# Seven output products of a conv-and-MLP block: 512 + 256 columns into one bank each, gate and residual in one VectorE step

## The chip, the cores and the metric

One Trainium2 core of one chip runs the whole block: batch 1, 256 tokens, model width 2048, all in float32. The metric is the device time of one execution in microseconds, as the median of several runs. Beside it a profiled execution of the same program is given; its span is counted from the first to the last instruction of the program.

## The reference

With depth 1 only the convolution mixer runs; the two attention mixers of the file are never called. Cut to what is computed:

```python
cond = silu(c)
sh1, sc1, g1, sh2, sc2, g2 = split(cond @ mod_w + mod_b, 6)
h = rms_norm(x, norm1_g) * (1 + sc1) + sh1
u = h @ conv_w_in + conv_b_in            # 2048 -> 4096
a, gt = split(u, 2);  u = a * sigmoid(gt)
u = causal depthwise convolution of 31 taps (u) + conv_dw_b
u = silu(layer_norm(u) * conv_ln_g + conv_ln_b)
y = u @ conv_w_out + conv_b_out          # 2048 -> 2048
x = x + (1 + g1) * y
h = rms_norm(x, norm2_g) * (1 + sc2) + sh2
x = x + (1 + g2) * (square(relu(h @ mlp_w1)) @ mlp_w2)
```

The change concerns the two lines with `conv_w_out` and `(1 + g1)`.

## The kernel before, in words

**Layout.** Activations are held transposed: 16 tiles of 128 channels by 256 tokens, two tiles to a "pair" (`k2`, eight pairs). A float32 operand is split into a rounded high part and the remainder, low part, both in the format `fp32r`. `hl[k2]` holds for each of its two tiles 512 columns: 256 of the high part, then 256 of the low part. A weight tile of 1 MB is split the same way into two halves, `hi` on ScalarE (L236) and `lo` on VectorE or GpSimd (L240). A product is then high·high + high·low + low·high.

**Jobs.** The block is a list of jobs: 16 `in` jobs (projection into the convolution), eight `out` jobs (the projection of the changed lines), then the MLP. Each `out` job makes two tiles of 128 output channels (`c` = 0, 1). The first, `out` 0, goes through the pairs in the outer loop (`mm_pair`, L283 to L286), so that it can start as soon as the first pair of the layer-normed activation exists, and it writes an `mm` tile of PSUM. The other seven take the function `mm` with `merged` true (L264 to L266): per tile and 128 input channels three products of 256 columns each, all added up in the same 256 columns. Both tiles of such a job share one `acc` tile of PSUM, a bank of 512 columns; there are two `acc` banks, so that one job can be read out while the next is computed. The `in` jobs and the first two `up` jobs use `mm` without `merged` (L268, L269): one product of 512 columns and one of 256 that is added to the second half, which leaves two halves to be added at the end.

**Evacuation of an `out` job (L1405 to L1416).** ScalarE applies gate and bias in place in PSUM, one instruction a tile (L1415: `acc` times the column `mcol(G1, k)` plus `gb`, where `gb` is the gate times `conv_b_out`). VectorE adds the 128x512 residual pair (L1416: `xp` = `acc` + `xp`). The residual `x` is loaded again for this (2 MB, key `("x", 0)`) when the memory of the convolution is free. Then ScalarE squares it (L1418), scales it into `a` (L1427), and `split_act` (L251 on ScalarE, L254 on VectorE) makes `xa[i]`, the operand of the first `up` jobs.

**What makes the operand.** In the stretch just before, ScalarE and VectorE turn the convolution's result into `hl`, pair by pair: VectorE L1386 multiplies by the inverse deviation, ScalarE L1390 applies the SiLU twice (one per tile), then the high part is copied (L251 on ScalarE, or L253 on VectorE for pairs 1 and 5) and VectorE makes the low part (L254).

**What sets the order.** Each engine works through its own list of instructions in order. The lists are written by a scheduler at build time, from its own estimate of times and from priorities: what is under `urgent()` goes ahead of what isn't, and `issue_after` names single instructions that must come first. So a change of the source can move instructions that it doesn't touch. Into the gaps of VectorE the scheduler puts the row sums of the SH2 modulation (L665, two per weight tile, against a copy of `cond` in PSUM) and the `lo` splits of the last `out` and the first `up` weights; GpSimd makes the `lo` parts of `out` 1 to 5.

**Loads.** All weight tiles go through SP's queue in one fixed order and land in seven `raw` buffers; a buffer is free again when its tile is split or summed.

Of the kernel before, what the change touches and what calls it, by code (L numbers as in the profile page):

```python
# [11 lines left out]
AF = mybir.ActivationFunctionType  # L12
ALU = mybir.AluOpType
# [3 lines left out]
T = 256  # L17
# [70 lines left out]
def conv_block(ctx: ExitStack, tc: tile.TileContext, x, vec, dwq, c_row, mod_r, mod_t, mod_c, w_first, w_in, w_out, w1, w2, out):  # L88
# [63 lines left out]
    def urgent():  # L152
        return tc.high_priority(offset=URGENT)
# [102 lines left out]
    def mm(p, c, key, acts_of, ks=range(KT), merged=False):  # L256
        halves = parts[key]
        for k in ks:
            hi, lo = halves[k // HALF]
            m = acts_of[k // 2][:, k % 2, :]  # L260
            if merged:
                out_p, begin, end = p[:, c, 0:T], k == 0, k == KT - 1
                w = hi[:, k % HALF, :]
                nc.tensor.matmul(out_p, w, m[:, 0:T], start=begin, stop=False)  # L264
                nc.tensor.matmul(out_p, w, m[:, T : 2 * T], start=False, stop=False)  # L265
                state["mm_end"] = nc.tensor.matmul(out_p, lo[:, k % HALF, :], m[:, 0:T], start=False, stop=end)  # L266
                continue
            nc.tensor.matmul(p[:, c, :], hi[:, k % HALF, :], m, start=(k == 0), stop=(k == KT - 1))  # L268
            state["mm_end"] = nc.tensor.matmul(  # L269
                p[:, c, T : 2 * T], lo[:, k % HALF, :], m[:, 0:T], start=False, stop=(k == KT - 1),  # L270
                skip_group_check=True,
            )
# [25 lines left out]
    def mm_tokens(sums, job, acts_of, last):  # L298
        steps = [(k, r) for k in range(HALF) for r in sums]
        if last:  # L300
            steps = [(k, r) for r in sums for k in range(HALF)]
        for k, (t, cs, p) in steps:
            hi, lo = [w[:, 4 * (k % 2) : 4 * (k % 2) + 4, :].rearrange("p k n -> p (k n)")[:, cs]
                      for w in parts[job + (k // 4,)][k // 2 % 2]]
            at = HALF * (job[2] % 2) + k
            m = acts_of[at // 2][:, at % 2, :]
            shared = job[0] == "down" and job[1] in EIGHT
            begin, end = at == 0 or shared and job[2] == 1 and t == 1 and at == HALF, at == KT - 1
            p_hi, p_lo = [m[:, n : n + P] for n in (t * P, T + t * P)]
            nc.tensor.matmul(p, p_hi, hi, start=begin, stop=False, skip_group_check=shared)  # L310
            nc.tensor.matmul(p, p_hi, lo, start=False, stop=False, skip_group_check=shared)  # L311
            nc.tensor.matmul(p, p_lo, hi, start=False, stop=end, skip_group_check=shared)  # L312

    def run_tasks():
        state["job"] += 1
        with tc.issue_after(state["w_lo"]), tc.issue_after(state["w_hi"]):
            for task in tasks.pop(state["job"], []):
                task()
# [371 lines left out]
    def mcol(which, k):  # L690
        return modc[:, which * KT + k : which * KT + k + 1]
# [21 lines left out]
    def ps_two():  # L713
        return ps.tile([P, 2, T], F32, name="acc", bufs=2)
# [90 lines left out]
    def splits(job):  # L805
        if job[0] == "eight":
            with urgent():
                split_eight(*job[1:])
            return
        if job[0] == "seven":  # L810
            with urgent():
                split_seven(*job[1:])
            return
        for c in range(2):
            if job + (c,) in parts_early:
                continue
            on_pool = job[0] == "in" or job in POOLED
            with urgent(), behind(c):
                split_w(job + (c,), nc.gpsimd if on_pool else nc.vector)
            if c == 0:  # L820
                state["next_hi"] = state["w_hi"]
                if job[0] in ("up", "down"):
                    with urgent():
                        run_tasks()

    def evac(p, cs=slice(0, 2), out=None):
        t1 = two()[:, cs, :]
# [347 lines left out]
    for n, job in enumerate(jobs):  # L1175
# [49 lines left out]
                    top_up()  # L1225
            continue
        if kind == "out" and i > 0:
            p = ps_two()
        elif not by_tokens(job):
            p = ps.tile([P, 2, 2 * T], F32, name="mm", bufs=2)  # L1230
        if by_tokens(job) and (i % 2 == 0 or kind == "down" and job[1] in EIGHT and i < 4):
# [2 lines left out]
        if job == ("up", 0, 0):  # L1234
            mm(p, 0, job + (0,), xa, range(SIDE))
            for at in range(2 * UNSCALED):
                shift_row(at, shown.pop(("up", 0, at // 2, at % 2)))
            fold_shift()
            mm(p, 0, job + (0,), xa, range(SIDE, KT))
            mm(p, 1, job + (1,), xa)  # L1240
        elif job == ("out", 0):
            for k2 in range(HALF):
                with tc.issue_after(state["row_end"].ins) if k2 == 1 else ExitStack():
                    mm_pair(p, job, k2)
                if k2 == 0:
                    with tc.issue_after(state["mm_end"].ins):
                        mod_chunk(*last_row[0][1:], last_row[1])
        elif job in K_OUTER:
            for k2 in range(HALF):
                for c in range(2):  # L1250
                    mm(p, c, job + (c,), xa if plain else hl, range(2 * k2, 2 * k2 + 2))
        elif kind == "in":
            rows = [key for key in after[job] if key[0] != "col"] if i < KT - 1 else []
            for c in range(2) if i < KT - 1 else (1, 0):
                for ks in (range(HALF), range(HALF, KT)):
                    with tc.issue_after(state.pop("rows_end")) if "rows_end" in state else ExitStack():
                        mm(p, c, job + (c,), hl, ks, i == KT - 1)
            if not CONV_AT.get(n):
                with tc.issue_after(state["mm_end"].ins):
                    mods(rows)  # L1260
                state["rows_end"] = state["row_end"].ins
        elif by_tokens(job):
            mm_tokens(sums[kind, i // 2], job, u2 if kind == "down" else hl, n == len(jobs) - 1)
        else:
            for c in range(2):
                mm(p, c, job + (c,), hl, merged=kind == "out")
        with tc.issue_after(state["mm_end"].ins) if kind == "in" else ExitStack():
            mod_finish()
        if n == KT - 3:
# [136 lines left out]
        if kind == "out":  # L1406
            if i == 0:
                xs = take(("x", 0))
            t2 = p[:, :, 0:T]
            xp = pair_of(xs, i)  # L1410
            with urgent():
                for c in range(2):
                    k = 2 * i + c
                    with tc.issue_after(state["next_hi"]) if i == HALF - 2 else ExitStack():
                        nc.scalar.activation(t2[:, c, :], t2[:, c, :], AF.Identity, scale=mcol(G1, k), bias=gb[:, k : k + 1])  # L1415
                nc.vector.tensor_tensor(xp, t2, xp, op=ALU.add)  # L1416
            ss = two()
            nc.scalar.activation(ss, xp, AF.Square)  # L1418
            if i == 0:
# [162 lines left out]
```

## Time and profile before

| | |
|---|---|
| runs | 1067.75 us median of 3 (1067.61 to 1067.9) |
| profiled execution | span 1065.8 us, 15587 instructions |
| median less span | 1.95 us, around the program's first and last instruction |
| HBM | 313.71 MB read, 17.83 MB written |
| `out` jobs 1 to 7 on TensorE | from 297.9 us; the three lines start 224 times each, the first at 297.8, the last at 380.5 us |
| end of the stage before (SiLU, L1390) | 14 instructions from 286.5 to 296.4 us |

The columns of the views are these. In the timeline: start and duration in us, engine, line, operation, tile written and tiles read, shape, count, and in brackets the idle time of the engine before it with what ended it. In the table by stretch: for each engine busy time and number of instructions, then the granted TensorE clock (1.00 is full), the share of time in which the DMA engines were busy, and GB/s. Durations of successive instructions overlap a little, on TensorE a great deal: what an instruction costs there is the distance between two starts. The names in the profile are those of the first tile in a buffer: a second use of the buffer of `x` is `x` too, and `u` stands for the operand of the MLP.

### The profile page before, as it was taken

Reading aid. Unit: us, or ns where it says so; the run is one execution under the profiler, and the core shown is the slowest. Engines: PE = TensorE matmul, PEld = TensorE weight load, DVE = VectorE, ACT = ScalarE, POOL = GpSimd, SP = SyncE. Lnnn points to the kernel's source line nnn. Section 1 sums busy time; section 2 is a strip of 40 time slices with the busy share of each in tenths; the row PEclk is TensorE's granted clock in tenths of the full one; section 3 lists DMA queues with packets and bytes.
Section 4 is the critical chain, followed back from the end, with each engine's and each line's share of the span. In section 5 each row is a group of like instructions: output and inputs, shape, how many; then the busy total and the mean of one; then the engine's idle time right before and its main releaser. Section 6 shows DMA issues by size and latency. Waiting matters only on the chain.

```text
span 1065.8 us, 15587 instructions
## 1 busy us (share of the span) xinstructions
PE 1048.6 (98%) x5844; PEld 867.4 (81%) x5844; DVE 911.9 (86%) x1176; ACT 609.0 (57%) x841; POOL 220.2 (21%) x153
## 2 busy tenths in 40 slices
PE   6999999999999999999999999999999999999998
PEld 3888886678699998888888888888888888888886
DVE  5767789998766889878879899899999899899896
ACT  4111298866775587444546575745566744657751
POOL 0000078989689262000000000000000000000001
PEclk8999999999999999999999999999999999999999
DMA  9999997997999977999994998693989795899753
GB/s 383 420 420 421 415 419 310 359 397 261 382 401 404 405 247 285 324 334 313 324 359 178 340 269 284 238 382 109 383 241 308 252 331 183 289 304 341 203 146 60
DMA packets 154334, 331.01 MB, mean 311 GB/s; under 512 B 88465, under 2 KB 114321, under 8 KB 119313
## 3 DMA queue, kind: packets, MB, share of 16 engines
q1 hardware_dynamic: 153248, 328.30, 84.8%
q0 software_dynamic: 864, 1.57, 1.1%
q8 instruction: 46, 0.75, 0.3%
q14 instruction: 30, 0.25, 0.1%
q10 hardware_dynamic: 146, 0.13, 0.0%
HBM read 313.71 MB, written 17.83 MB: 311 GB/s over the span
## 4 chain that ended last, share of the span: by engine, by line
PE 83%; DMA 10%; DVE 5%; ACT 1%; issue 1%; SPq 0%; DVEq 0%; ACTq 0%
PE mm L312 12%; PE mm L310 12%; PE mm L311 12%; DMA raw<-mod_c 9%; PE mm L268 6%; PE mm L269 3%; PE acc L265 3%; PE acc L264 3%; PE acc L266 3%; PE mm L1090 2%; PE row L576 2%; PE acc L485 2%; PE acc L486 2%; PE acc L484 1%; DVE raw L669 1%; DVE lo L240 1%
## 5 line engine op out<-in xcount | busy, mean ns | idle before, releaser
L236 ACT ACTIVATE hi<-raw 128x1024 fp32r<-128x1024 f32 x374 | 384.8, 1055 | 258.2 <-PE mm L312 127.6
L240 DVE TENSOR_TENSOR lo<-raw,hi 128x1024 fp32r<-128x1024 f32 x313 | 371.7, 1219 | 52.6 <-ACT hi L236 51.4
L240 POOL TENSOR_TENSOR lo<-raw,hi 128x1024 fp32r<-128x1024 f32 x61 | 153.6, 2549 | 31.1 <-ACT hi L236 31.1
L669 DVE SCALAR_TENSOR_TENSOR raw<-raw,cond 128x2048 f32<-128x2048 f32 x50 | 117.7, 2356 | 27.0 <-DMA raw<-mod_c 26.9
L460 POOL DMA_DIRECT2D out<-two x6 | 5.4, 902 | 641.6 <-DVE two L458 632.3
L311 PE MATMUL mm<-lo,u 128*128 128x512 f32 x320 | 124.5, 389 | 0.0
L312 PE MATMUL mm<-hi,u 128*128 128x512 f32 x320 | 124.0, 389 | 0.0
L310 PE MATMUL mm<-hi,u 128*128 128x512 f32 x320 | 123.8, 389 | 0.0
L312 PE MATMUL mm<-hi,hl 128*128 128x512 f32 x288 | 112.1, 389 | 0.0
L311 PE MATMUL mm<-lo,hl 128*128 128x512 f32 x288 | 112.0, 389 | 0.0
L310 PE MATMUL mm<-hi,hl 128*128 128x512 f32 x288 | 112.0, 389 | 0.0
L969 DVE SCALAR_TENSOR_TENSOR acc<-u,v,acc 128x256 f32<-128x256 f32 x230 | 91.5, 482 | 0.0
L268 PE MATMUL mm<-hl,hi 128*128 128x512 f32 x224 | 80.0, 401 | 0.0
L311 PEld LDWEIGHTS mm<-lo,u 128*128 128x128 f32 x320 | 60.1, 188 | 12.6
L312 PEld LDWEIGHTS mm<-hi,u 128*128 128x128 f32 x320 | 60.1, 188 | 12.5
L310 PEld LDWEIGHTS mm<-hi,u 128*128 128x128 f32 x320 | 60.1, 188 | 12.4
L873 PE MATMUL mm<-two,first 128*128 128x256 f32 x240 | 57.0, 392 | 8.5 <-ACT two L931 8.5
L264 PE MATMUL acc<-hl,hi 128*128 128x256 f32 x224 | 63.4, 283 | 0.0
L265 PE MATMUL acc<-hl,hi 128*128 128x256 f32 x224 | 63.4, 283 | 0.0
L266 PE MATMUL acc<-hl,lo 128*128 128x256 f32 x224 | 63.4, 283 | 0.0
L312 PEld LDWEIGHTS mm<-hi,hl 128*128 128x128 f32 x288 | 54.1, 188 | 11.3
L311 PEld LDWEIGHTS mm<-lo,hl 128*128 128x128 f32 x288 | 54.1, 188 | 11.2
(381 smaller groups left out, 2059.2 us busy)
## 6 DMA issues: line engine op xcount, KB each, us to landing
raw<-w SPq DMA_DIRECT2D x128, 1024.0 KB, 7.3
raw<-mod_c SPq DMA_DIRECT2D x64, 1024.0 KB, 9.7
raw<-mod_r SPq DMA_DIRECT2D x28, 1024.0 KB, 8.8
raw<-w_in SPq DMA_DIRECT2D x16, 1024.0 KB, 10.5
raw<-w_out SPq DMA_DIRECT2D x16, 1024.0 KB, 8.0
first<-w_first SPq DMA_DIRECT2D x15, 1024.0 KB, 19.8
u<-kept SPq DMA_DIRECT2D x24, 512.0 KB, 7.6
flat<-two SPq DMA_DIRECT2D x30, 256.0 KB, 6.9
```

The lines of the kernel that those rows point to most:

```text
L236: state["w_hi"] = nc.scalar.activation(hi, w[:, ks, :], AF.Copy).ins
L240: end = by.tensor_tensor(lo, w[:, ks, :], hi.bitcast(F32), op=ALU.subtract)
L264: nc.tensor.matmul(out_p, w, m[:, 0:T], start=begin, stop=False)
L265: nc.tensor.matmul(out_p, w, m[:, T : 2 * T], start=False, stop=False)
L266: state["mm_end"] = nc.tensor.matmul(out_p, lo[:, k % HALF, :], m[:, 0:T], start=False, stop=end)
L268: nc.tensor.matmul(p[:, c, :], hi[:, k % HALF, :], m, start=(k == 0), stop=(k == KT - 1))
L310: nc.tensor.matmul(p, p_hi, hi, start=begin, stop=False, skip_group_check=shared)
L311: nc.tensor.matmul(p, p_hi, lo, start=False, stop=False, skip_group_check=shared)
L312: nc.tensor.matmul(p, p_lo, hi, start=False, stop=end, skip_group_check=shared)
L669: end = nc.vector.scalar_tensor_tensor(w, w, 1.0, cb, op0=ALU.mult, op1=ALU.mult, accum_out=acc)
L873: step = nc.tensor.matmul(held[n][:, c, :], w[:, 2 * n + c, :], h, start=k == 0 and c == 0, stop=k == KT - 1, skip_group_check=True)
L969: end = nc.vector.scalar_tensor_tensor(out, s, w, acc, op0=ALU.mult, op1=ALU.add)
```

## The change

The seven jobs `out` 1 to 7 no longer use the merged form. Each tile gets an `acc` bank of its own (so a job takes both banks), filled by one product of 512 columns and one of 256. VectorE then reads both halves: two instructions a tile, four a job, each of 128x256, that multiply a half with the gate column as scalar and add it to the residual. The bias part of the sum goes into the residual ahead of time: ScalarE adds `gb` to the fourteen tiles of `x` that belong to these jobs, in fourteen instructions of 128x256 written at `out` 0 to `out` 6, outside `urgent()`. `out` 0 keeps its evacuation. The name `next_hi`, with which the evacuation of `out` 6 was held back, goes away.

```diff
-            if c == 0:
-                state["next_hi"] = state["w_hi"]
-                if job[0] in ("up", "down"):
-                    with urgent():
-                        run_tasks()
+            if c == 0 and job[0] in ("up", "down"):
+                with urgent():
+                    run_tasks()
...
         if kind == "out" and i > 0:
-            p = ps_two()
+            p = [ps_two().rearrange("p a t -> p (a t)")[:, None, :] for _ in range(2)]
...
+        elif kind == "out":
+            for c in range(2):
+                mm(p[c], 0, job + (c,), hl)
         else:
             for c in range(2):
-                mm(p, c, job + (c,), hl, merged=kind == "out")
+                mm(p, c, job + (c,), hl)
...
-            t2 = p[:, :, 0:T]
             xp = pair_of(xs, i)
+            for c in range(2) if i + 1 < HALF else ():
+                k = 2 * i + 2 + c
+                x_next = pair_of(xs, i + 1)[:, c, :]
+                nc.scalar.activation(x_next, x_next, AF.Identity, bias=gb[:, k : k + 1])
             with urgent():
-                for c in range(2):
-                    k = 2 * i + c
-                    with tc.issue_after(state["next_hi"]) if i == HALF - 2 else ExitStack():
-                        nc.scalar.activation(t2[:, c, :], t2[:, c, :], AF.Identity, scale=mcol(G1, k), bias=gb[:, k : k + 1])
-                nc.vector.tensor_tensor(xp, t2, xp, op=ALU.add)
+                if i == 0:
+                    t2 = p[:, :, 0:T]
+                    for c in range(2):
+                        nc.scalar.activation(t2[:, c, :], t2[:, c, :], AF.Identity, scale=mcol(G1, c), bias=gb[:, c : c + 1])
+                    nc.vector.tensor_tensor(xp, t2, xp, op=ALU.add)
+                for c in range(2) if i else ():
+                    for a in range(2):
+                        nc.vector.scalar_tensor_tensor(
+                            xp[:, c, :], p[c][:, 0, T * a : T * a + T], mcol(G1, 2 * i + c), xp[:, c, :],
+                            op0=ALU.mult, op1=ALU.add,
+                        )
```

In the lists of the engines this moves instructions at two places that matter here. In the rows, a number behind a name tells one tile from another, `x1` is the residual that was loaded again, `hl_2621`, `hl_2630`, `hl_2648` are the activation's pairs 3, 4 and 6, `acc_2625` is the SiLU of pair 4, and xN is a count.

ScalarE, where the activation's pairs are made, before:

```order
L1390 ACTIVATE acc_2616<-two_2615,v_72 128x256 x2
L251 ACTIVATE hl_2621<-acc_2616 128x2x256
L1390 ACTIVATE acc_2625<-two_2624,v_72 128x256 x2
L251 ACTIVATE hl_2630<-acc_2625 128x2x256
L1390 ACTIVATE acc_2634<-two_2633,v_72 128x256 x2
L1390 ACTIVATE acc_2643<-two_2642,v_72 128x256 x2
L251 ACTIVATE hl_2648<-acc_2643 128x2x256
```

ScalarE, the same place in the change (L1391 is the SiLU now, L1414 the new bias step):

```order
L1391 ACTIVATE acc_2616<-two_2615,v_72 128x256 x2
L251 ACTIVATE hl_2621<-acc_2616 128x2x256
L1391 ACTIVATE acc_2625<-two_2624,v_72 128x256
L1414 ACTIVATE x1_2504<-x1_2504,gb_2501 128x256 x4
L1391 ACTIVATE acc_2625<-two_2624,v_72 128x256
L1414 ACTIVATE x1_2504<-x1_2504,gb_2501 128x256 x10
L251 ACTIVATE hl_2630<-acc_2625 128x2x256
L1391 ACTIVATE acc_2634<-two_2633,v_72 128x256 x2
L1391 ACTIVATE acc_2643<-two_2642,v_72 128x256 x2
L251 ACTIVATE hl_2648<-acc_2643 128x2x256
```

All fourteen bias steps stand in one place, ahead of the high part of pair 4 and of all that is made after it.

VectorE, around the evacuation of the fifth merged job (`out` 5), before; the three sums of the SH2 modulation around it are two rows each:

```order
L665 SCALAR_TENSOR_TENSOR raw_3226,modc_116<-raw_3226,mm_2942 128x1024
L665 SCALAR_TENSOR_TENSOR raw_3226,rest2_2502<-raw_3226,mm_2944 128x1024
L1416 TENSOR_TENSOR x1_2504<-acc_3392,x1_2504 128x512
L665 SCALAR_TENSOR_TENSOR raw_3230,modc_116<-raw_3230,mm_2942 128x1024
L665 SCALAR_TENSOR_TENSOR raw_3230,rest2_2502<-raw_3230,mm_2944 128x1024
L254 TENSOR_TENSOR u2_3499<-two_3496,u2_3499 128x2x256
L665 SCALAR_TENSOR_TENSOR raw_3240,modc_116<-raw_3240,mm_2942 128x1024
L665 SCALAR_TENSOR_TENSOR raw_3240,rest2_2502<-raw_3240,mm_2944 128x1024
```

VectorE, the same sums in the change, with the evacuation of the second tile of `out` 5 (`acc_3283`) among them:

```order
L665 SCALAR_TENSOR_TENSOR raw_3144,modc_116<-raw_3144,mm_2916 128x1024
L665 SCALAR_TENSOR_TENSOR raw_3144,rest2_2502<-raw_3144,mm_2918 128x1024
L665 SCALAR_TENSOR_TENSOR raw_3148,modc_116<-raw_3148,mm_2916 128x1024
L665 SCALAR_TENSOR_TENSOR raw_3148,rest2_2502<-raw_3148,mm_2918 128x1024
L1423 SCALAR_TENSOR_TENSOR x1_2504<-acc_3283,modc_116,x1_2504 128x256
L665 SCALAR_TENSOR_TENSOR raw_3158,modc_116<-raw_3158,mm_2916 128x1024
L665 SCALAR_TENSOR_TENSOR raw_3158,rest2_2502<-raw_3158,mm_2918 128x1024
L1423 SCALAR_TENSOR_TENSOR x1_2504<-acc_3283,modc_116,x1_2504 128x256
```

The two halves of one bank are now taken with two sums between them, and two whole sums stand ahead of the first.

## The prediction

> **What bounds the kernel now.** I read the page first, then the table by stretch, then the chain of waits and the timelines around the `out` jobs.
>
> ```profile
> PE 1048.6 (98%) x5844; PEld 867.4 (81%) x5844; DVE 911.9 (86%) x1176; ACT 609.0 (57%) x841; POOL 220.2 (21%) x153
> PE 83%; DMA 10%; DVE 5%; ACT 1%; issue 1%; SPq 0%; DVEq 0%; ACTq 0%
> ```
>
> TensorE is busy 98% of the span and carries 83% of the chain that ends last. The table by stretch says whether that holds where the change works and behind it (columns: stretch, length, then PE, PEld, DVE, ACT, POOL busy, clock, DMA share, GB/s):
>
> ```profile
> 305.00:316.00 11.00, 11.00 (x94) 11.00 (x94) 6.58 (x18) 10.21 (x15) 11.00 (x5) 1.00 0.96 386
> 328.00:340.00 12.00, 12.00 (x103) 12.00 (x102) 7.78 (x12) 7.22 (x12) 12.00 (x8) 1.00 1.00 406
> 352.00:364.00 12.00, 12.00 (x103) 12.00 (x102) 11.41 (x17) 7.55 (x11) 1.49 (x2) 1.00 1.02 421
> 364.00:376.00 12.00, 12.00 (x103) 12.00 (x102) 8.57 (x9) 6.36 (x11) 2.64 (x2) 1.00 0.82 311
> 400.00:1060.00 660.00, 659.83 (x2919) 545.25 (x2918) 590.18 (x605) 379.39 (x440) 12.66 (x9) 1.00 0.82 273
> ```
>
> In the `out` jobs TensorE never idles, and from 400 to 1060 us it idles 0.17 us. So a microsecond that TensorE gains or loses at the `out` jobs reaches the end whole: no later wait gives it back. VectorE is nearly full in one stretch (11.41 of 12).
>
> Just ahead of this, where the activation's pairs are made, the chain leaves TensorE. Its rows (start, length, what) and the start of pair 4 on TensorE:
>
> ```profile
> 291.42 0.47 ACT acc L1390
> 291.91 0.58 ACT acc L1390
> 292.51 0.60 ACT hl L251
> ...
> 294.21 0.70 DVE hl L253
> 294.95 0.39 PE mm L285
> ```
> ```profile
> 293.21 0.34 PE L285 MATMUL mm<-hl,hi 128*128 128x256 f32 x1
> ```
>
> ScalarE finishes the high part of pair 4 at 292.51 + 0.60 = 293.11, and TensorE starts pair 4 at 293.21. There is no slack there: ScalarE sets TensorE's pace, and pair 5 waits again, until 294.95.
>
> **The change, part by part.**
>
> *1. The products.* Six steps of the unmerged form in an `in` job and later in an `up` job, and one step of the merged form:
>
> ```profile
> 230.05 0.40 PE L268 MATMUL mm<-hl,hi 128*128 128x512 f32 x1
> ...
> 232.17 0.40 PE L268 MATMUL mm<-hl,hi 128*128 128x512 f32 x1
> ```
> ```profile
> 399.85 0.39 PE L268 MATMUL mm<-u,hi 128*128 128x512 f32 x1
> ...
> 401.93 0.39 PE L268 MATMUL mm<-u,hi 128*128 128x512 f32 x1
> ```
> ```profile
> 300.09 0.28 PE L264 MATMUL acc<-hl,hi 128*128 128x256 f32 x1
> ...
> 300.45 0.28 PE L264 MATMUL acc<-hl,hi 128*128 128x256 f32 x1
> ```
>
> Merged, a step costs 0.360 us; unmerged 2.12 / 6 = 0.353 in the `in` job, 2.08 / 6 = 0.347 in the `up` job. The columns streamed are the same 768; only one instruction's fixed part goes. There are 7 jobs x 2 tiles x 16 steps = 224, so the saving is 224 x 0.0067 = **1.5 us**, or 3.0 at the `up` job's pace. I take 1.5: the `in` jobs run with the same operand `hl`. As bounds, a gain of 0 (the new first step of each bank may lag) to 3.0.
> The Trainium skill, "TensorE: Matmul & The Clock Gate", Part 1, gives a back-to-back distance of N / 2.4 GHz plus a fixed 2.5 ns or so; by that, one matmul fewer saves 224 x 2.5 ns = 0.56 us, an estimate from that page. The rows here show more for a 256-column product (0.120 us against that page's 0.109), so the rows stand.
>
> *2. The fourteen bias steps.* They stand in ScalarE's list between the two SiLUs of pair 4 and its high part, and they need the residual and `gb`:
>
> ```profile
> 282.25 0.37 SPq L212 DMA_DIRECT2D x<-x  x1
> ```
> ```profile
> x<-x SPq DMA_DIRECT2D x1, 2048.0 KB, 12.5
> ```
> ```profile
> L1356 DVE TENSOR_TENSOR gb<-modc,v x1: 175/175/175, 278.3 to 278.3; 128x16 f32<-128x16 f32 x1
> ```
> ```profile
> 335.02 1.11 ACT L1415 ACTIVATE acc<-acc,gb,modc 128x256 f32<-128x256 f32 x2 [4.72 <-PE acc L266]
> 336.06 1.05 ACT L236 ACTIVATE hi<-raw 128x1024 fp32r<-128x1024 f32 x1
> ```
> ```profile
> 319.17 0.90 ACT L1427 ACTIVATE two<-x,amp 128x256 f32<-128x256 f32 x2
> ```
>
> `gb` is there at 278.5. The load of `x` is issued at 282.25 and lands 12.5 us later, at 294.75. Nothing ahead of that differs between the two programs' lists, so I keep this time. ScalarE waits in order: at 335.02 it had stood 4.72 us for a product, with weight splits queued behind. So it reaches the first bias step at 291.9 and stands until 294.8, with pair 4's second SiLU, its high part, pairs 5 to 7, the next weights' `hi` parts (for which GpSimd waits) and the copy of `cond` queued behind.
>
> Then the price of the steps. The same shape on the same tile, L1427, takes 0.90 us for two with 0.495 each, so 0.405 from start to start. Four steps end at 294.8 + 1.6 = 296.4, the SiLU takes 0.58, ten more take 4.05: pair 4's high part starts at 301.1 instead of 292.5. **TensorE stands 8.6 us longer.** If a step costs as L1415 does (1.11 for two, 0.56 apart), 14 x 0.155 = 2.2 us more. Below, it is 14 x 0.405 + 0.1 = 5.8, if `x` had landed before 291.9. TensorE has no other work to take meanwhile: its list goes on with pairs 4, 5 and 6, and only then with `out` 1.
>
> *3. The clock after that stand.* The only long idle time of TensorE in this trace, and the stretches behind it:
>
> ```profile
> 19.71 5.71 PE L873 MATMUL mm<-two,first 128*128 128x256 f32 x16 [4.69 <-ACT two L931]
> ```
> ```profile
> 17.00:19.70 2.70, 0.00 (x0) 0.00 (x0) 2.50 (x8) 0.61 (x2) 0.00 (x0) 0.50 1.01 419
> 19.70:23.80 4.10, 4.09 (x10) 3.28 (x11) 4.06 (x5) 0.41 (x1) 0.00 (x0) 0.50 1.01 422
> 23.80:27.00 3.20, 3.20 (x17) 2.81 (x16) 1.35 (x4) 1.02 (x2) 0.00 (x0) 1.00 1.00 417
> ```
>
> After 4.69 us without work the granted clock was 0.50, and it stayed there for 4.1 us of work (10 matmuls in 4.10 us, then 17 in 3.20). An idle time of over 8 us should do the same: half of 4.1 us is lost, 2.05. Of that, the 0.3 us by which pair 5 waited before is covered now: **+1.7 us**. Bounds: 0 to 3.
> The Trainium skill states the rule behind it ("TensorE: Matmul & The Clock Gate", Part 1: after an idle window of about 3.4 us the clock halves, and comes back after about as long of sustained work); this trace agrees with 4.69 us idle and 0.50 granted.
>
> *4. Evacuation.* Out go fourteen L1415 and seven L1416; in come 28 VectorE steps. The nearest row with PSUM in, a scalar column and SBUF in is L1108:
>
> ```profile
> L1108 DVE SCALAR_TENSOR_TENSOR u<-mm,v,two 128x256 f32<-128x256 f32 x12 | 5.7, 481 | 3.3 <-ACT two L1106 3.2
> L1416 DVE TENSOR_TENSOR x<-acc,x 128x512 f32<-128x512 f32 x7 | 4.8, 686 | 6.3 <-ACT acc L1415 6.3
> L665 DVE SCALAR_TENSOR_TENSOR raw<-raw,mm 128x1024 f32<-128x1024 f32 x24 | 28.1, 1211 | 2.5 <-ACT mm L1437 2.5
> ```
>
> 28 x 0.481 - 7 x 0.686 = 8.7 us more on VectorE, which has 0.6 to 4.4 us free in the stretches above. A job now holds both banks, so the next job's first tile can start only when this job's first tile is read out, half a job (16 x 0.353 = 5.7 us) after its end. Mostly that is enough. The place to fear is `out` 5's second tile: ahead of its first half stand two sums of two rows (4 x 1.2), and between its halves another (2 x 1.2). My count, an estimate on the times of the trace before: VectorE reads `out` 5's first tile at 352 to 354 between splits, starts the sums at about 356, and with 4 x 1.15 + 0.4 + 2 x 1.15 + 0.4 = 7.7 us (rows overlap a little) frees the bank at 363.7. The merged products end at 380.8, and a job took 96 x 0.120 = 11.5, so the second tile of `out` 6 began at 380.8 - 1.5 x 11.5 = 363.5, and at the new pace wants its bank some 0.7 sooner. Behind the waiting instruction stand the `lo` splits of `out` 7 and the first `up` job, with the same small reserve at `out` 6's second tile. I take **+0.8 us** for these waits, with 0 (the loads run ahead during the stand, so sums start earlier) and 3 (each of three tiles late by a whole 1.2 us sum) as bounds. ScalarE's 14 x 0.53 us fewer are off the path: they were covered by TensorE's 100%.
>
> *Sum:* -1.5 + 8.6 + 1.7 + 0.8 = +9.6 us. On the profiled span, 1065.8 + 9.6 = 1075.4; 1.95 us lie around the span (1067.75 - 1065.8), so **1077.3 us**, 0.9% slower.
>
> **The rivals.**
> - *ScalarE has room after all: faster.* If TensorE still gets pair 4 by 293.2, only the products count: 1067.75 - 1.5 = 1066.3. It decides at 291.9: `x` would have to land before it, and 5.7 us of reserve would have to lie between ScalarE and pair 4. For it speaks that ScalarE is busy 57% over all; against it the 0.10 us between 293.11 and 293.21, and the 12.5 us of the load. 4%. A half-way house (`x` early and half of the steps covered, +3 - 1.5) ends within 0.2%: 4%.
> - *The stand, but at full clock.* 1077.3 - 1.7 = 1075.6. For: only one such row in the trace. Against: that row, at half the idle time. 18%.
> - *VectorE becomes the bound.* If in every job both late banks cost a sum (14 x 1.2 less the reserve), 5 to 10 us come on top: 1082 to 1087. For: 11.41 of 12 us busy in one stretch and 8.7 us more work. Against: GpSimd's contention-free stretch after 352, and loads that have run ahead. 8%.
> - *Forecast*, the sum as it stands: 66%.
>
> **How the numbers follow.** Lowest: gain 3.0, stand 8.0 (`x` landing 0.6 us sooner), clock 0, waits 0: +5.0, 1072.8. Highest: gain 0, stand 10.8, clock 1.7, waits 2: +14.5, 1082.2. That range holds the forecast, the full-clock rival and a little of the third. A measurement can tell about 0.2% (2.1 us) from no change. Slower by more: 66 + 18 + 8 = 92%; within: 4%; faster: 4%.
>
> **What would show it.** Right: fourteen L1414 in one row of ScalarE with the first waiting about 2.9 us for `x`; an idle time of some 8.5 us on TensorE before pair 4, named after `hl`; a clock below 1.00 in the 4 us after it; `out` steps of 0.353 us; idle times under 1 us on TensorE at the second tiles of `out` 6 and 7. Wrong: TensorE at pair 4 by 294, or `x` landing elsewhere than at 295; or steps of L1423 far from 0.48 us, or idle time of TensorE at every change of bank; or idle time behind 400 us, where I count none.

## The result, and the profile after

| | before | after |
|---|---|---|
| median | 1067.75 us (1067.34 to 1067.9, five runs) | 1077.97 us (1077.44 to 1087.58, five runs) |
| ratio after / before | | 1.0111, 95% interval 1.0094 to 1.0128 |
| span of the profiled execution | 1065.8 us | 1085.8 us |

The changed kernel is 1.1% slower. Its profiled execution happens to be the longest of the five; the spans of the other four are 1075.7 to 1076.2 us. It holds two events, one that comes back in the second profile of this kernel (e0) and one that doesn't, and they must be read apart. The page (busy times, then the shares of the chain that ended last):

```profile
PE 1050.9 (97%) x5620; PEld 858.1 (79%) x5620; DVE 932.4 (86%) x1197; ACT 607.2 (56%) x841; POOL 220.1 (20%) x153
PE 79%; DVE 9%; DMA 9%; ACT 1%; issue 1%; POOL 0%; SPq 0%; DVEq 0%; ACTq 0%
```

TensorE has 224 products fewer and is nevertheless busy 2.3 us longer, and the chain has moved 4 points from TensorE to VectorE. The timelines of ScalarE where the activation's pairs are made, and of TensorE at pair 4 and at `out` 3's first tile, in this execution:

```profile
291.22 0.56 ACT L1391 ACTIVATE acc<-two,v 128x256 f32<-128x256 f32 x1
294.70 1.70 ACT L1414 ACTIVATE x<-x,gb 128x256 f32<-128x256 f32 x4 [2.91 <-DMA x<-x]
296.31 0.55 ACT L1391 ACTIVATE acc<-two,v 128x256 f32<-128x256 f32 x1
296.80 4.08 ACT L1414 ACTIVATE x<-x,gb 128x256 f32<-128x256 f32 x10
```
```profile
301.41 0.58 PE L285 MATMUL mm<-hl,hi 128*128 128x256 f32 x1 [8.14 <-ACT hl L251]
...
340.99 0.76 PE L268 MATMUL acc<-hl,hi 128*128 128x512 f32 x1 [8.72 <-DVE x L1423]
```

The first idle time is the one that was forecast: ScalarE waits 2.91 us for the residual, then makes fourteen bias steps, and TensorE gets pair 4 at 301.41 instead of 293.21. The second, at 340.99, is the extra of this execution. The table by stretch shows what each does to the clock (the number before the DMA share):

```profile
293.00:301.40 8.40, 0.27 (x3) 0.07 (x1) 0.01 (x1) 6.70 (x17) 0.00 (x0) 0.78 1.02 422
301.40:304.50 3.10, 3.09 (x14) 3.09 (x15) 2.40 (x4) 3.00 (x6) 0.00 (x0) 0.51 1.00 418
304.50:308.00 3.50, 3.50 (x29) 3.41 (x28) 0.36 (x1) 3.47 (x6) 1.74 (x1) 1.00 0.82 335
...
332.30:341.00 8.70, 0.01 (x1) 0.04 (x1) 8.70 (x5) 1.00 (x1) 6.61 (x4) 0.67 0.52 217
341.00:345.40 4.40, 4.40 (x14) 3.72 (x15) 4.37 (x9) 1.33 (x3) 0.00 (x0) 0.50 0.30 56
```

After each of the two idle times TensorE works 3.1 to 4.4 us at half clock: 14 matmuls in 3.09 us, then 29 in 3.50. In the stretch 332.30 to 341.00 VectorE is busy for all 8.70 us, with five instructions. What they are stands in the timelines of VectorE and GpSimd of this execution:

```profile
325.85 13.61 DVE L254 TENSOR_TENSOR u<-two,u 128x512 fp32r<-128x512 f32 x1
339.38 0.47 DVE L1423 SCALAR_TENSOR_TENSOR x<-acc,modc,x 128x256 f32<-128x256 f32 x1
```
```profile
325.82 4.79 POOL L240 TENSOR_TENSOR lo<-raw,hi 128x1024 fp32r<-128x1024 f32 x2
330.55 0.76 POOL L1433 TENSOR_TENSOR sqacc<-sqacc,two 128x256 f32<-128x256 f32 x1
331.25 4.68 POOL L240 TENSOR_TENSOR lo<-raw,hi 128x1024 fp32r<-128x1024 f32 x2
335.87 0.74 POOL L1433 TENSOR_TENSOR sqacc<-sqacc,two 128x256 f32<-128x256 f32 x1
336.55 2.36 POOL L240 TENSOR_TENSOR lo<-raw,hi 128x1024 fp32r<-128x1024 f32 x1
```

The low part of an MLP operand (L254) lies on VectorE for 13.61 us, as long as GpSimd works without a pause, from 325.82 to 338.91; the next L254, at 339.77 with GpSimd idle, takes 0.67 us. Behind the long one in VectorE's list stands the evacuation (L1423) of `out` 2's first tile, and TensorE wants its bank for `out` 3. To read the change without this event, the same kernel was run again.

### The profile page after: what moved, and what is told of

The parts are those of the page before. It is cut to its first block, busy times and chain, and to the rows that moved or that the text cites. A ratio compares the mean times of both kernels' runs of the same rounds, so it can differ in the third digit from the quotient of the medians.

```text
span 1085.8 us, 15148 instructions
## 1 busy us (share of the span) xinstructions
PE 1050.9 (97%) x5620; PEld 858.1 (79%) x5620; DVE 932.4 (86%) x1197; ACT 607.2 (56%) x841; POOL 220.1 (20%) x153
## 4 chain that ended last, share of the span: by engine, by line
PE 79%; DVE 9%; DMA 9%; ACT 1%; issue 1%; POOL 0%; SPq 0%; DVEq 0%; ACTq 0%
PE mm L312 12%; PE mm L310 12%; PE mm L311 12%; DMA raw<-mod_c 7%; PE mm L268 6%; PE mm L269 3%; PE acc L268 2%; DVE lo L240 2%; PE mm L1088 2%; DVE raw L669 2%; PE row L576 2%; DVE u L254 2%; PE acc L485 2%; PE acc L486 2%; PE acc L484 1%
## 5 line engine op out<-in xcount | busy, mean ns | idle before, releaser
L669 DVE SCALAR_TENSOR_TENSOR raw<-raw,cond 128x2048 f32<-128x2048 f32 x50 | 115.3, 2307 | 28.1 <-DMA raw<-mod_c 28.1
L310 PE MATMUL mm<-hi,u 128*128 128x512 f32 x320 | 123.9, 389 | 0.0
L310 PE MATMUL mm<-hi,hl 128*128 128x512 f32 x288 | 112.1, 389 | 0.0
L268 PE MATMUL acc<-hl,hi 128*128 128x512 f32 x224 | 80.7, 404 | 9.2 <-DVE x L1423 9.2
L310 PEld LDWEIGHTS mm<-hi,u 128*128 128x128 f32 x320 | 60.1, 188 | 12.5
L269 PE MATMUL mm<-hl,lo 128*128 128x256 f32 x224 | 62.9, 281 | 0.0
```

Of the source, the lines that this page charges most:

```text
L269: state["mm_end"] = nc.tensor.matmul(p[:, c, T : 2 * T], lo[:, k % HALF, :], m[:, 0:T], start=False, stop=(k == KT - 1), skip_group_check= ...
L669: end = nc.vector.scalar_tensor_tensor(w, w, 1.0, cb, op0=ALU.mult, op1=ALU.mult, accum_out=acc)
```

## The experiments

The stand is TensorE's idle time ahead of pair 4. Theory A, that of the prediction: the loss is ScalarE's list (the wait for the residual, then 14 x 0.405 us) plus the half clock behind it; the products gain a little, and VectorE's lateness takes back part. Rival B: the two banks and VectorE's extra work cost the time. Rival C: the stand costs its length, at full clock. Theory V is about the end of the stage: what the products gain is lost there, because VectorE's list has no reserve.

All traces are cut at the same instants of TensorE: pair 4's start (prediction), the first product of `out` 1, and the first L310, a matmul of the next form behind the first `up` jobs. Times in us; the medians of e5 and e7 are from a second group of runs, in which before measured 1067.5, those of e9 and e10 from a third, with 1067.77.

| kernel | pair 4 starts | to `out` 1 | `out` 1 to L310 | L310 to the end | span | median |
|---|---|---|---|---|---|---|
| before | 293.21 | 4.72 | 111.28 | 656.6 | 1065.8 | 1067.96 |
| e0, the change again | 301.20 | 6.71 | 111.78 | 656.6 | 1076.3 | 1078.04 |
| e1, steps behind | 293.26 | 4.75 | 111.45 | 656.5 | 1066.0 | 1067.81 |
| e2, steps alone | 300.80 | 6.99 | 111.28 | 656.6 | 1075.7 | 1077.52 |
| e4, stand filled | 301.28 | 4.77 | 112.02 | 656.5 | 1074.6 | 1076.29 |
| e5, `lo` first | 293.18 | 4.72 | 114.57 | 657.3 | 1069.8 | 1072.39 |
| e7, six steps | 297.30 | 6.86 | 115.71 | 656.6 | 1076.5 | 1078.79 |
| e9, two merged | 293.45 | 4.46 | 110.21 | 656.7 | 1064.8 | 1066.54 |
| e10, four merged | 293.32 | 4.72 | 110.64 | 657.4 | 1066.1 | 1067.9 |

**e0_again**: the changed kernel, without an edit.

> The changed kernel once more, for a profile and more executions. Theory A (ScalarE's list): every execution has an idle time of TensorE of about 8.1 us ahead of pair 4, so nothing comes in near 1067.75; the executions gather at 1077 to 1078. Theory S (GpSimd keeps VectorE out now and then): about one execution in five is some 10 us longer, and where a profile has such an execution, one L254 of over 5 us stands in it; where it hasn't, no L254 is over 3 us and TensorE's second long idle time is missing. Rival B (the evacuation is what costs): idle times at the changes of bank add up to 8 us or more in every execution.

Measured: 1078.04 us (1076.69 to 1079.58, five runs), ratio 1.0093 (1.0079 to 1.0107). TensorE's idle times in this trace:

```profile
301.20 0.58 PE L285 MATMUL mm<-hl,hi 128*128 128x256 f32 x1 [8.00 <-ACT hl L251]
...
373.16 0.47 PE L268 MATMUL acc<-hl,hi 128*128 128x512 f32 x1 [0.47 <-DVE x L1423]
...
396.26 1.29 PE L600 MATMUL row<-raw,shz 128*32 128x128 f32 x36 [0.32 <-ACT shz L1459]
397.71 0.70 PE L695 MATMUL small<-two,ones 128*128 128x256 f32 x2 [0.17 <-ACT two L1428]
```

ScalarE's first bias step and, behind the fourteenth, pair 4's high part:

```profile
294.49 1.70 ACT L1414 ACTIVATE x<-x,gb 128x256 f32<-128x256 f32 x4 [2.75 <-DMA x<-x]
...
300.58 0.57 ACT L251 ACTIVATE hl<-acc 128x512 fp32r<-128x512 f32 x1
```

There are no 8.72 us this time. The same L254 got through at GpSimd's first change of instruction (VectorE's timeline, then four stretches: the one behind the stand, two that answer to those shown of before, the stage being about 10 us later here, and the rest of the program):

```profile
326.59 2.95 DVE L254 TENSOR_TENSOR u<-two,u 128x512 fp32r<-128x512 f32 x1
```
```profile
301.20:306.40 5.20, 5.20 (x24) 5.20 (x25) 2.75 (x4) 5.07 (x9) 0.36 (x1) 0.50 1.00 414
...
352.00:364.00 12.00, 12.00 (x70) 10.40 (x69) 11.08 (x15) 6.20 (x8) 10.01 (x7) 1.00 1.01 420
364.00:376.00 12.00, 11.53 (x66) 9.79 (x65) 12.00 (x21) 5.08 (x7) 2.10 (x2) 1.00 1.01 413
410.00:1070.00 660.00, 659.83 (x2920) 545.33 (x2919) 589.12 (x603) 379.11 (x440) 14.26 (x10) 1.00 0.82 273
```

So without that event the cost is 10.5 us of span: 8.0 at the start of pair 4, 2.0 from there to `out` 1, 0.5 up to L310, nothing behind it. The 2.0, the half clock, isn't the same each time: it lasts 5.2 us behind pair 4 here and 3.1 in the first profile, where pair 4 to `out` 1 took 307.16 - 301.41 = 5.75 us, 1.0 more than before. VectorE is busy for all 12.00 us where TensorE wants `out` 6's second tile.

**e1_bias_behind**: the changed kernel with each pair's steps held behind the last high part that ScalarE has made. They then start at 300.8 us and later, and nothing of pairs 4 to 7 has to wait for them.

```diff
-                nc.scalar.activation(x_next, x_next, AF.Identity, bias=gb[:, k : k + 1])
+                with tc.issue_after(state["hi_end"]):
+                    nc.scalar.activation(x_next, x_next, AF.Identity, bias=gb[:, k : k + 1])
```

> The changed kernel with one edit: each pair's two bias steps are issued behind the last high part that ScalarE made (the activation's pair 7, then the operand of the job before), so none stands ahead of pairs 4 to 7. Theory A: the stand (8.1 us) and the slow clock behind it go, no idle time ahead of pair 4 beyond 0.4 us, and the time is that of before less the 1.5 us of the products plus the waits at the banks: 1066 to 1068. Rival B: the time stays at 1073 or more, with idle times at the changes of bank. Theory S: a tail of some 10 us may still come in single executions, since GpSimd's and VectorE's work overlap as before.

Measured: 1067.81 us (1067.57 to 1069.19, 11 runs), ratio 0.9999 (0.999 to 1.0007). Pair 4 starts at 293.26 and there is no drop of the clock: the place of the steps is worth the whole loss. What is left of the change is level with before, and the trace says why. The first product of `out` 1 and, 192 steps on, that of `out` 7, then the one idle time behind it:

```profile
298.01 0.40 PE L268 MATMUL acc<-hl,hi 128*128 128x512 f32 x1
...
368.17 0.40 PE L268 MATMUL acc<-hl,hi 128*128 128x512 f32 x1
...
370.05 0.39 PE L269 MATMUL acc<-hl,lo 128*128 128x256 f32 x1 [1.48 <-DVE lo L240]
```
```profile
368.38 0.48 DVE L1424 SCALAR_TENSOR_TENSOR x<-acc,modc,x 128x256 f32<-128x256 f32 x1 [1.70 <-PE acc L269]
368.78 1.22 DVE L240 TENSOR_TENSOR lo<-raw,hi 128x1024 fp32r<-128x1024 f32 x1
```

Six jobs take 70.16 us; before they take 71.45 (297.93 to 369.38), so the products gain 1.29 over 192 steps, 0.0067 each. Then VectorE (second fence) stands 1.70 us for the end of `out` 6's second tile, and the `lo` part that `out` 7 needs is queued behind that evacuation: 1.48 us of TensorE.

**e2_bias_alone**: the kernel before with only the fourteen steps added; the gate stays on ScalarE, without the bias.

```diff
+            for c in range(2) if i + 1 < HALF else ():
+                k = 2 * i + 2 + c
+                x_next = pair_of(xs, i + 1)[:, c, :]
+                nc.scalar.activation(x_next, x_next, AF.Identity, bias=gb[:, k : k + 1])
...
-                        nc.scalar.activation(t2[:, c, :], t2[:, c, :], AF.Identity, scale=mcol(G1, k), bias=gb[:, k : k + 1])
+                        if i == 0:
+                            nc.scalar.activation(t2[:, c, :], t2[:, c, :], AF.Identity, scale=mcol(G1, k), bias=gb[:, k : k + 1])
+                        else:
+                            nc.scalar.activation(t2[:, c, :], t2[:, c, :], AF.Copy, scale=mcol(G1, k))
```

> The kernel before with one part of the change alone: the fourteen bias steps (they land at the same place of ScalarE's list as in the change), and the gate on ScalarE without bias. Products, banks and the VectorE step stay those of before. Theory A: the stand and the slow clock come in full, without the gain of 1.5 us: 1077.5 to 1079.5, an idle time of 8.1 us ahead of pair 4 and a clock of 0.50 after it. Rival B: within 1 us of before, 1067 to 1069.

Measured: 1077.52 us (1076.69 to 1078.11, four runs), ratio 1.0085 (1.0072 to 1.0099): without banks, without VectorE's steps and with the merged products, nearly the whole loss. Rival B falls.

```profile
300.80 0.58 PE L285 MATMUL mm<-hl,hi 128*128 128x256 f32 x1 [7.49 <-ACT hl L251]
```

Its stand is 7.49 us where 8.1 was expected: `x` let ScalarE go at 294.09 here, at 294.70 in the first profile of the change. From `out` 1 to L310 this kernel takes 111.28 us, exactly as before.

**e4_busy_stand**: the changed kernel with 64 more products of 256 columns between pairs 3 and 4, so that TensorE works through the stand. They overwrite half of the first output tile's sum, which is read later (the expectation has that wrong), so the run is of use for its times alone.

```diff
+                    if k2 == 4:
+                        w_hi = parts[job + (0,)][0][0]
+                        for n in range(64):
+                            with tc.issue_after(state["mm_end"].ins):
+                                state["mm_end"] = nc.tensor.matmul(
+                                    p[:, 0, T : 2 * T], w_hi[:, n % HALF, :], hl[3][:, 0, 0:T], start=True, stop=True, skip_group_check=True
+                                )
+                    with tc.issue_after(state["mm_end"].ins) if k2 >= 4 else ExitStack():
+                        mm_pair(p, job, k2)
```

> The changed kernel with 64 matmuls of 256 columns more, between pairs 3 and 4, into a half of the bank that nothing reads: 64 x 0.120 = 7.7 us of work inside the stand of 8.1 us. It parts the two terms of the stand. Theory A with the clock: TensorE isn't idle for over 0.7 us, the clock stays at 1.00, and the time is 1.3 to 2 us under that of the changed kernel. If the clock costs nothing beside the stand: the same time within 0.5 us. Rival B: longer by up to 7.7 us, since TensorE would only get more work.

Measured: 1076.29 us (1076.19 to 1078.14, five runs), ratio 1.0078 (1.0065 to 1.009). The table by stretch:

```profile
293.00:301.20 8.20, 8.13 (x68) 7.92 (x67) 0.00 (x0) 6.66 (x17) 0.00 (x0) 1.00 1.00 416
301.20:306.00 4.80, 4.63 (x36) 4.43 (x37) 2.77 (x4) 4.67 (x10) 0.00 (x0) 1.00 1.02 425
```

Pair 4 starts as late as in e0 (301.28), the clock is 1.00 throughout, and 36 matmuls go into the 4.80 us behind it where e0 has 24 in 5.20. The clock's share is 1078.04 - 1076.29 = 1.75 us by the medians; by the traces 6.71 - 4.77 = 1.94 from pair 4 to `out` 1. Rival C falls, and so does rival B, for which this run had to be longer.

**e7_six_steps**: the changed kernel with only the steps of `out` 0 to 2 left in their place.

```diff
-                nc.scalar.activation(x_next, x_next, AF.Identity, bias=gb[:, k : k + 1])
+                with tc.issue_after(state["hi_end"]) if i > 2 else ExitStack():
+                    nc.scalar.activation(x_next, x_next, AF.Identity, bias=gb[:, k : k + 1])
```

> The changed kernel with six of the fourteen bias steps (those of `out` 0 to 2) where they were, and the other eight held behind the last high part of the activation. Theory A (the stand of TensorE before pair 4 is the wait for the load of x plus 0.405 us for each step): 8 x 0.405 = 3.2 us off the stand of 8.0, so some 4.8 us idle, still a clock of 0.50 behind it (4.69 us idle did that early in this program), and 1074.5 to 1075.2 us; if the clock holds at 4.8 us idle, 1.75 less. Rival L (nearly all of the stand is the wait for the load, the steps run beside something else): stand over 7 us, 1077 to 1078 us. Rival S (only the steps count, the load is there): stand under 3 us, under 1072 us.

Measured: 1078.79 us (1075.96 to 1079.43, four runs), ratio 1.0098 (1.0083 to 1.0112): no better than with all fourteen. The stand itself did as theory A says. ScalarE, then TensorE:

```profile
293.78 1.70 ACT L1415 ACTIVATE x<-x,gb 128x256 f32<-128x256 f32 x4 [2.02 <-DMA x<-x]
295.39 0.55 ACT L1391 ACTIVATE acc<-two,v 128x256 f32<-128x256 f32 x1
295.88 0.89 ACT L1415 ACTIVATE x<-x,gb 128x256 f32<-128x256 f32 x2
```
```profile
297.30 0.58 PE L285 MATMUL mm<-hl,hi 128*128 128x256 f32 x1 [4.05 <-ACT hl L251]
...
395.31 0.79 PE L695 MATMUL small<-two,ones 128*128 128x256 f32 x1 [3.37 <-ACT two L1429]
```

From the first step to pair 4 it takes 297.30 - 293.78 = 3.52 us, with fourteen steps 301.41 - 294.70 = 6.71: 3.19 for eight steps, 0.40 each (`x` landed 0.9 us earlier here, hence 4.05). What was won came back 98 us later, as 3.37 us of waiting for a square that waits for VectorE, and a second half-clock stretch behind it. So the expectation's time is a miss by some 4 us, although what it says of the stand holds. VectorE ahead of that wait:

```profile
382.51 2.34 DVE L240 TENSOR_TENSOR lo<-raw,hi 128x1024 fp32r<-128x1024 f32 x2
...
385.17 4.55 DVE L240 TENSOR_TENSOR lo<-raw,hi 128x1024 fp32r<-128x1024 f32 x2
389.64 0.47 DVE L1424 SCALAR_TENSOR_TENSOR x<-acc,modc,x 128x256 f32<-128x256 f32 x1
390.04 4.10 DVE L669 SCALAR_TENSOR_TENSOR raw<-raw,cond 128x2048 f32<-128x2048 f32 x1
```

Two splits take 4.55 us instead of 2.34, and a sum (L669) 4.10 where the median of the 50 in this trace is 2.29. Both overlap with GpSimd's work on two splits of its own, from 385.49 to 391.99. Together that is 4.0 us of lateness, more than the 3.37 that TensorE stood; this is read from the trace, no run takes GpSimd's splits away.

**e5_lo_first**: e1 with the evacuation of `out` 6's second tile held behind the `lo` splits of `out` 7.

```diff
+                    with tc.issue_after(state["w_lo"]) if i == HALF - 2 and c else ExitStack():
+                        for a in range(2):
+                            nc.vector.scalar_tensor_tensor(
...
```

> The changed kernel with two edits: the fourteen bias steps are held behind the last high part of the activation (as in e1_bias_behind), and the evacuation of the second tile of `out` 6 is held behind the `lo` splits of `out` 7's weights on VectorE. e1 stood level with before although its steps cost 0.353 us instead of 0.360; its trace has one idle time of 1.48 us on TensorE, at the first low product of `out` 7, which waits for that `lo`. Theory V (the products do gain about 1.3 us, and VectorE's order at the end of the stage gives it back): the 1.48 us goes, and nothing above 0.7 us takes its place; 1066.3 to 1066.9 us, 0.1 to 0.15% faster than before. Theory B (VectorE has too much to do there, and whichever of its instructions stands last is late): the idle time moves to the first `up` job or to the second tile of `out` 7, 1 to 2 us; 1067.5 to 1068.5 us, level with before.

Measured: 1072.39 us (1071.62 to 1077.83, six runs), ratio 1.0052 (1.0036 to 1.0067): theory V in this form is refuted, and theory B's time (1067.5 to 1068.5) is missed by 4 us too. The 1.48 us are gone, but TensorE stands 3.07 us at the first `up` job. That wait, then VectorE ahead of it, then the stretch in which it falls:

```profile
387.88 0.50 PE L268 MATMUL mm<-u,hi 128*128 128x512 f32 x1 [3.07 <-DVE u L254]
```
```profile
371.43 2.28 DVE L669 SCALAR_TENSOR_TENSOR raw<-raw,cond 128x2048 f32<-128x2048 f32 x1
...
374.94 5.75 DVE L240 TENSOR_TENSOR lo<-raw,hi 128x1024 fp32r<-128x1024 f32 x4
380.61 4.47 DVE L669 SCALAR_TENSOR_TENSOR raw<-raw,cond 128x2048 f32<-128x2048 f32 x1
...
385.01 2.81 DVE L254 TENSOR_TENSOR u<-two,u 128x512 fp32r<-128x512 f32 x1
```
```profile
380.00:387.50 7.50, 4.80 (x28) 3.92 (x26) 7.50 (x4) 1.41 (x2) 6.74 (x2) 1.00 0.21 45
```

The low part of the operand (L254) stands behind four splits and a sum, so it is VectorE's list that is late, at the place that theory B named. But the list alone doesn't account for it. The sum takes 4.47 us here and 2.28 at 371.43, L254 takes 2.81 where it needs 0.67 alone: 4.3 us more, while GpSimd works for 6.74 us on two splits (the stretch 380.00 to 387.50). In e1 GpSimd's splits start at 387.15, behind the same two instructions, which take 2.28 and 0.69. So the 3.07 us are explained by VectorE's order meeting GpSimd's work, not by the order alone. This is read from the traces; no run takes GpSimd's splits away.

**e9_two_merged**: e1 with `out` 6 and 7 as before: merged products, one bank a job, gate and bias on ScalarE, one addition on VectorE.

```diff
+        if kind == "out" and i >= 6:
+            p = ps_two()
...
-                mm(p, c, job + (c,), hl)
+                mm(p, c, job + (c,), hl, merged=kind == "out")
...
-                if i == 0:
+                if i == 0 or i >= 6:
...
```

> The changed kernel with the bias steps held behind the last high part of the activation (as in e1_bias_behind), and with `out` 6 and 7 as before: merged products, one bank a job, gate and bias on ScalarE and one addition on VectorE. `out` 1 to 5 keep the change. e5_lo_first had shown that moving VectorE's order at the end of the stage only moves its lateness (3.07 us at the first `up` job). Theory V (the products' gain is real and is lost only because the evacuation of the last two jobs stands in VectorE's way where it has no reserve): ten halves at 5.65 instead of 5.76 us, 1.1 us, are kept, no idle time over 0.5 us on TensorE in this stage, 1066.4 to 1066.8 us, about 0.1% faster than before. Theory B (VectorE's work over the whole stage is what is late, wherever it is put): an idle time of 0.5 to 3 us at `out` 6, 7 or the first `up` job, 1067.0 to 1070 us.

Measured: 1066.54 us (1066.29 to 1067.33, 11 runs), ratio 0.9988 (0.9979 to 0.9997): faster than both kernels, by 0.12% than before. The first L310 of this kernel, then that of before:

```profile
408.12 0.39 PE L310 MATMUL mm<-hi,hl 128*128 128x512 f32 x1
```
```profile
409.21 0.39 PE L310 MATMUL mm<-hi,hl 128*128 128x512 f32 x1
```

From `out` 1 to there 110.21 us instead of 111.28: 1.07, which is ten halves at 16 x 0.0067. TensorE has no idle time of 0.15 us or more from `out` 1 to L310. In e9 VectorE spends 2 x 0.686 on the two evacuations that take it 8 x 0.477 in the change, 2.4 us less. GpSimd's and VectorE's instructions stand at the end of the stage as they do before the change, so this run doesn't tell the saved time from the older order.

**e10_four_merged**: the same with the limit at 4, so that only `out` 1 to 3 keep the change.

> As e9_two_merged, but `out` 4 to 7 are as before and only `out` 1 to 3 keep the change. Theory V: six halves at 5.65 instead of 5.76, 0.65 us kept, 1066.8 to 1067.2 us, a little behind e9. Theory B: less of VectorE's work than in e9, so less idle time than there; if e9 loses 1 us or more, this one is faster than e9.

Measured: 1067.9 us (1067.0 to 1069.69, 11 runs), ratio 1.0001 (0.9992 to 1.001). In its trace the stage gained as expected, L310 at 408.68 with `out` 1 at 298.04, 0.64 us. But this execution waits later, in a part of the MLP that no edit touches:

```profile
978.82 0.50 PE L312 MATMUL mm<-hi,u 128*128 128x512 f32 x1 [0.59 <-DVE u L254]
```

So the expected time (1066.8 to 1067.2) is missed by the median, and three of the eleven runs lie in it; what makes the others later, and whether it is this wait, is open.

## Why the prediction was right

The forecast was 1077.3 us, the result 1077.97, by the mechanism that was named: e1 and e2 show the place of the steps, e4 the clock. That the number fits to 0.7 us is in part luck, since a stand that was counted 0.6 us too long and waits that were counted 1.2 us too short offset each other. Its terms against what the runs showed:

| step of the prediction | predicted | measured |
|---|---|---|
| products | -1.5 | -1.29 over 192 steps (e1), so -1.5 over 224 |
| stand before pair 4 | +8.6 | +8.2 (first profile), +8.0 (e0), +7.6 (e2) |
| clock behind it | +1.7 | +1.0 (first profile), +2.0 (e0), +2.3 (e2); +1.75 by e4's median |
| waits for banks and VectorE | +0.8 | +2.0 (e0) |
| sum | +9.6 | +10.5 (e0's span), +10.2 (medians) |

- **The stand** was 0.6 us shorter: the load let ScalarE go at 294.49 (e0) where 294.8 had been counted, and from there to the high part it took 300.58 - 294.49 = 6.1 us instead of 6.3.
- **The clock** was right in kind; e4 shows it by taking away the idle time alone. Its size is no fixed price: one kernel showed 1.0 and 2.0 us in its two profiles, after idle times of 8.14 and 8.00 us, so the 1.7 lies between by chance.
- **The products** were right: the `in` jobs' pace, 0.353, is that of the changed `out` jobs in e1. The `up` jobs' pace, the other bound, occurs too: in the first profile each 16 steps behind the 8.72 us take 5.55 us, 0.347 a step, for five tiles. Why there are two paces is open.
- **The waits** are the term that was mis-sized, by 1.2 us. "I take +0.8 us for these waits" counted late evacuations of `out` 5's and 6's second tiles, for which TensorE waits at the second tiles of `out` 6 and 7. Only the first showed, with 0.47 us (e0), and more was lost where nothing had been counted: behind `out` 7, where ScalarE's `shz` and the last square wait for VectorE (0.32 + 0.17 us idle). The 2.0 is a difference, 111.78 - 111.28 + 1.5. Cut in e0's trace at the end of the last `out` product (393.24; before, 380.90), 0.8 of it falls on the `out` jobs and 1.2 behind them (3.07 us of `up` products that were done ahead are counted with the second part). Behind them VectorE's L254 at 390.77 takes 2.88 us and L1458 at 393.57, an instruction of 128x16, takes 2.37, while GpSimd works on two splits from 390.29 to 395.91: the same meeting as in e5 and e7, which the prediction had put at nothing.
- **The sign "idle behind 400 us, where I count none"** held: 0.17 us idle in 660, as before. But "a microsecond that TensorE gains or loses at the `out` jobs reaches the end whole" holds for a loss only as far as these runs go: in e7 most of a gain of 4 us ahead of the `out` jobs was lost again before 400.
- **The rival in which VectorE becomes the bound** was given 8%, and as an account of the median it is wrong. But its time, 1082 to 1087, is nearly what the profiled execution took (1087.58), by another way: one long wait of VectorE, not a late bank in every job. And "GpSimd's contention-free stretch after 352" was no argument against it: the 8.72 us came ahead of 352, while GpSimd was busy, and in e0, where the stage is later, GpSimd is busy for 10.01 of the 12 us from 352 to 364. A time that long was seen in one of the ten executions of this kernel (after and e0). That the wait goes by GpSimd's pauses is read from one trace and was not provoked by a run; what decides whether L254 gets through at the first change of instruction or at none of the first six is open.

## What to carry to other kernels

Instructions that are written "outside urgent" still stand in an in-order list: look at which tile they wait for and what is queued behind them; here a whole 10 us hung on the place of fourteen instructions of 0.4 us (e1). An engine that is 86% busy over the program may have no reserve in one stage, and there an order that mends one wait makes the next (e5), and a shorter stand upstream is not a shorter time (e7). Look then not only at the engine's list but at what GpSimd does in the same microseconds: in both runs VectorE's own instructions had grown by 4.0 to 4.3 us. What helped was to leave the last two jobs as they were (e9). If one profiled execution stands apart from the other times, profile the same kernel again before reading causes from it.

## What the runs showed of the hardware

**A VectorE instruction with two SBUF operands can be kept out much longer than one GpSimd instruction.** 13.61 us in the change's trace against 2.95 in e0's for the same instruction, both while GpSimd worked. The Trainium skill, "SBUF — State Buffer", section "SBUF: two separate sides", says that an instruction of VectorE with two SBUF inputs and a GpSimd instruction that reads SBUF exclude each other, and that the loser is blocked for the winner's whole instruction. The 2.95 us agrees; the 13.61 us, six changes of instruction on GpSimd long, goes beyond it. In two further traces a sum of 2.28 us took 4.47 (e5) and 4.10 (e7) beside GpSimd's splits.

**An idle time of 3.37 us was enough to halve the clock, and the halving doesn't always last equally long.** In e5 TensorE stood 3.07 us and then worked at full clock; in e7 it stood 3.37 us, from 391.94, and the clock was halved from 395.02 for 3.4 us. The stretches behind the two (e5, then e7):

```profile
387.88:391.30 3.42, 3.42 (x49) 2.50 (x53) 0.86 (x3) 2.70 (x6) 0.01 (x1) 1.00 0.55 184
```
```profile
395.02:398.44 3.42, 3.13 (x28) 2.22 (x32) 0.78 (x1) 3.38 (x8) 1.25 (x1) 0.50 0.85 302
```

The rule that the prediction cited from the Trainium skill, "TensorE: Matmul & The Clock Gate", Part 1 (about 3.4 us of idling), fits e5; in e7 the clock had fallen 3.1 us into the idle time, a little sooner than that. After the stand of about 8 us the half clock outlasted the idle time by 3.1 us in one execution and by 5.2 in the other (first profile and e0).
